# A hybrid decoder block on one core: every large SBUF tile moved to an address that is a multiple of 512 bytes

## The chip, the core and the metric

The kernel runs on 1 core of one Trainium2 chip (trn2). The metric is device microseconds of one execution. TensorE (PE) multiplies, VectorE (DVE) and ScalarE (ACT) prepare operands and empty PSUM, GpSimd (POOL) and SyncE (SP) mostly issue DMAs. SBUF has 128 partitions; a tile takes the same byte range in each of them, and "address" below is the byte offset in a partition.

## What is computed

The reference, cut to what matters (256 tokens, model width 4096):

```python
h = rmsnorm(x, norm_w)
proj = h @ w_in                                   # (256, 4096) x (4096, 20480)
u_p, z_p, u_c, b_c, c_c, z_c, g_logit = split(proj)
y_pool = causal_multiscale_pool(u_p, pool_w, pool_scale) * silu(z_p)
y_conv = b_c * conv3(c_c * u_c) * silu(z_c)
br = stack([y_pool, y_conv]) @ w_branch           # two products (256, 2048) x (2048, 4096)
merged = sum(sigmoid(g_logit + gate_b) * br)
out = rmsnorm(x + merged @ w_out, final_norm_w)
```

Everything is float32 in and out. The weights, 446 loads of 1 MB each, are read once.

## The kernel before, in words

**Precision.** Each operand is split in two float32r parts, a high part (the rounded value) and a low part (the rest). A product of two float32 matrices is three matmuls: high x high, high x low, low x high. Each matmul has a 128x128 float32r stationary operand (512 bytes per partition, loaded by its own weight-load instruction, PEld in the profile) and a 128x512 float32r moving operand (2,048 bytes per partition).

**Units and steps.** The work is a list of units of 1,024 output columns: 20 units over `w_in` (units `c..`, `p..`, `g..`), 8 over `w_branch` (`b..`), 4 over `w_out` (`o..`). A unit is a list of steps of 256 rows of contraction; each step loads one 1 MB weight block. A step is of kind P (plain: 8 products, 24 matmuls) or S (a Strassen-like scheme with 7 products, 21 matmuls, for which VectorE makes sums of weight quarters). A string such as `TEN` or `NINE` (lines 34 to 49) gives a unit's kinds in order. Two more kinds, B and M, serve the causal pooling.

**The tiles that matter here.**

- `raw` (line 100): three slots of 8 KB, the weight blocks as they come from HBM through SP's queue.
- `ring` (line 99): 15 cells of 4 KB, each a high and a low half of 2,048 bytes. ACT writes the high half (`highs`, line 223), DVE the low half (`lows`, line 227), from `raw` or from `parts`. Matmuls read `ring` as the moving operand.
- `parts` (line 1136): the sums of quarters of an S step, made by DVE.
- `arena` (line 98): the stationary operands, in entries of 512 bytes (`Operand`, line 167). What does not fit there lies in three other tiles: `last_pair` (the pair of rows that is `LAST`, line 144), `side` (the first four S entries of a pair that is held as a P operand but that some units use in an S step, line 193) and, in the first unit alone, `extra` (line 138).
- `E` and `Y` (lines 101, 102): results of a unit on their way through sums, gates and transposes; `sa` and `sb` scratch; `ident` the identity for transposes; `bands`, `edge` the moving operands of the pooling matmuls, with `cnt` and `ic` their counts; small tables `par`, `rin`, `rout`, `ssq`, `ossq`.

**Order.** All engines run in the order in which the program is written (`pin`, line 57). While the matmuls of step i are issued (`multiply`, line 1020), the preparations of up to four later steps are issued between them (`pump`, line 987), as far as `raw` slots and `ring` cells are free; results of the unit before come one piece at a time (`tick`, line 1013). A matmul waits for its ring cell and, for the first product into a PSUM bank, for the bank to have been emptied; ACT waits for a ring cell to be released by the matmuls that read it; DVE waits for ACT's high half.

**Placement.** SBUF pools are stacks from the two ends. Pool `const` (line 89) takes tiles from the left end, which begins at 16,512 behind a reserved stretch and four constants; pool `upper` (line 90) from the right end, which lies at 229,344. `opening`, `parts`, `side`, `bands`, `more` are opened behind `const` one after another, `last` (which holds `last_pair`) left of `upper`. Each tile is rounded up to 32 bytes. Nothing in the kernel states an address; they follow from the order in which tiles are made.

Of the kernel before, what the change touches and what calls it, by code (L numbers as in the profile page):

```python
# [9 lines left out]
F32 = mybir.dt.float32  # L10
F32R = mybir.dt.float32r
# [4 lines left out]
P = 128  # L16
T = 256
D = 4096
HALF = D // 2
NU = 1024  # L20
NH = 512
EPS = 1e-6
WINDOWS = (2, 4, 8, 16)
KB = 256

ND, NS, NB = 8, 6, 2
CELLS = 15
NRAW = 3
# [24 lines left out]
def hybrid_block(ctx: ExitStack, tc: tile.TileContext, x, xc, prm, rows_in, w_in, pool_w, w_branch, w_out, out):  # L53
# [5 lines left out]
    def act(dst, src, func=AF.Copy, **kw):  # L59
        return pin(nc.scalar.activation(dst, src, func, **kw))  # L60
# [4 lines left out]
    def mul(dst, a, b):  # L65
        return tt(dst, a, b, ALU.mult)
# [16 lines left out]
    def move(dst, src):  # L83
        return pin(nc.gpsimd.dma_start(dst, src))
# [5 lines left out]
    upper = ctx.enter_context(tc.tile_pool(name="upper", bufs=1, side="right"))  # L90
# [2 lines left out]
    dram = ctx.enter_context(tc.tile_pool(name="dram", bufs=1, space=bass.MemoryType.DRAM))  # L93

    def sb(name, shape, dt=F32):
        return const.tile(shape, dt, name=name)

    arena = sb("arena", [P, (4 * ND + 7 * NS + 8 * (NB - 1)) * KB], F32R)
    ring = sb("ring", [P, CELLS, 2, NH], F32R)
    raw = upper.tile([P, NRAW, 2 * NU], F32, name="raw")  # L100
    E = sb("E", [P, 2, NU])
    Y = upper.tile([P, 2, NU], F32, name="Y")
    sa = sb("sa", [P, 8, P])
    ident = sb("ident", [P, P])
    par = sb("par", [P, 112])
    rin = sb("rin", [P, 3])
    rout = sb("rout", [P, 2])
    ssq = sb("ssq", [P, 2, 4])
    ossq = sb("ossq", [P, 2, 5])

    PE_ = [[psum.tile([P, NH], F32, name=f"sums{t}{n}") for n in range(2)] for t in range(2)]
    PF = [psum.tile([P, NH], F32, name=f"shared{i}") for i in range(4)]
# [28 lines left out]
    band_pool = {}  # L141
# [81 lines left out]
    def highs(cells, src):  # L223
        for i, c in runs(cells):
            act(ring[:, c, 0], src[:, i])

    def lows(cells, src):
        for i, c in runs(cells):
            sub(ring[:, c, 1], src[:, i], ring[:, c, 0].bitcast(F32))

    def high(cell, a=0, b=NH):
        return ring[:, cell, 0, a:b]

    def low(cell, a=0, b=NH):
        return ring[:, cell, 1, a:b]

    def quarters(tile_):
        return tile_.rearrange("p a (b c) -> p (a b) c", c=NH)

    class Step:  # L240
# [28 lines left out]
        def rest(self):  # L269
# [32 lines left out]
            if self.kind == "B":  # L302
                def parts(cells):
                    self.cells = cells
                    highs(cells, quarters(E))
                    lows(cells, quarters(E))

                return [(4, lambda: self.unit.flags.get("base"), parts)]

            def pooled(cells):  # L310
                self.pool_cells = cells
                q = quarters(E)[:, 2 * self.g:2 * self.g + 2]
                highs(cells, q)
# [5 lines left out]
        def groups(self):  # L319
            gs = []  # L320
            if self is steps[0]:
                for k in (1, 0):
                    for n in (1, 0):
                        cell = self.cells[2 * (1 - k) + 1 - n]
                        h, l = high(cell), low(cell)
                        for i in range(3):
                            for t in range(2):
                                ah, al = self.op.standing(k, t)
                                gs.append([("E", t, n), [((ah, h), (al, h), (ah, l))[i]], ()])
                        gs[-1][2] = [cell]  # L330
            elif self.kind == "P":
                for k in (1, 0):
                    for n in reversed(self.halves):
                        cell = self.cells[2 * (1 - k) + 1 - n]
                        for t in self.toks:
                            ah, al = self.op.standing(k, t)
                            gs.append([("E", t, n), [(ah, high(cell)), (ah, low(cell)), (al, high(cell))], ()])
                        if self.final:
                            gs[-1][2] = [cell]
            else:  # L340
                d, w = self.cells, self.sum_cells
                prods = {"M1": (A11, d[2], ("F", 0, 0)),
                         "N3": (Q3, d[1], ("E", 0, 0)),
                         "M2": (A12, d[0], ("E", 0, 1)),
# [107 lines left out]
    def transposes(src, done):  # L452
        items = []
        for j in range(4):
            def f(j=j):
                for i in range(2):
                    for t in range(2):
                        c = (2 * j + i) * P
                        pin(nc.tensor.transpose(shared(j)[:, i * T + t * P:i * T + (t + 1) * P],  # L459
                                                src[:, t, c:c + P], ident))  # L460
                done(j)
            items.append(f)
        return items
# [4 lines left out]
    def put(dst, src):  # L468
        for k in range(2):
            move(dst[:, :, 1 - k], src.rearrange("p (q k) t -> p q k t", k=2)[:, :, k])  # L470

    def chan(tile_):
        return tile_.rearrange("p a n -> p (a n)").rearrange("p (b t) -> p b t", t=T)

    def bankview(j):
        return shared(j).rearrange("p (b t) -> p b t", t=T)

    def gap(n):
        return [None] * n
# [38 lines left out]
    def in_unit(name, col, epi, text, **kw):  # L518
        units.append(Unit(name, lambda i: w_in[col // NU, i], seq_x(text), x_ops, epi, scaled=True, **kw))
        units[-1].text = text  # L520
        return units[-1]
# [15 lines left out]
    def silu_y(late):  # L537
        def silu(t):
            act(Y[:, t], Y[:, t], AF.Silu, **(dict(scale=rin[:, t:t + 1]) if late else {}))
        return gap(18 if late else 3) + [lambda: silu(0), None, lambda: silu(1)]  # L540
# [5 lines left out]
    def conv_units(c, first):  # L546
        base = 2 * HALF + c * NU

        def b_epi(u):
            def copy(j):  # L550
                act(chan(Y)[:, 2 * j:2 * j + 2], bankview(j))
            return gap(6) + transposes(E, copy) + [lambda: move(g_d[c], Y)]

        def c_epi(u):
# [5 lines left out]
            def taps(j):  # L560
                v, y = chan(E)[:, 2 * j:2 * j + 2], chan(Y)
                for i in range(2):
                    b = 2 * j + i
                    kb = 8 * c + b
                    act(y[:, b], v[:, i], AF.Identity, scale=tap_col(2, kb), bias=bias_col(kb))
                for s in (1, 2):
                    for i in range(2):
                        b = 2 * j + i
                        kb = 8 * c + b
                        stt(y[:, b, s:], v[:, i, 0:T - s], tap_col(2 - s, kb), y[:, b, s:], ALU.mult, ALU.add)  # L570

            items = gap(6) + pairs(transposes(E, copy)) + gap(1)
            for j, n in enumerate((1, 7, 8, 8)):
                items += gap(n) + [lambda j=j: taps(j)]
            return items + [lambda: move(E, g_d[c])] + gap(6) + [lambda: mul(E, E, Y), lambda: put(y_d[1, c], chan(E))]

        u = in_unit(f"cz{c}", base + 3 * HALF, lambda u: silu_y(u.late) + (gap(4) + side_items(ND - 1) if first else []),
                    FIRST if first else SIX4, dst=Y)
        u.rotates, u.late = first, not first
# [10 lines left out]
    def band_items(c):  # L590
        if c == 0:
            side["stack"].close()
            pool = bands_open.enter_context(tc.tile_pool(name="bands", bufs=1))
            band_pool.update(cnt=pool.tile([P, 2], F32, name="cnt"),
                             bands=pool.tile([P, 2, T], F32R, name="bands"),
                             edge=pool.tile([P, 2, P], F32R, name="edge"),
                             ic=pool.tile([P, 16], F32, name="ic"))
            for t in range(16):
                pin(nc.gpsimd.memset(band_pool["ic"][:, t:t + 1], 1.0 / (t + 1)))
        cnt, bands, edge = (band_pool[k] for k in ("cnt", "bands", "edge"))  # L600

        def scratch(g):
            return sa[:, 4 + 2 * g:6 + 2 * g].rearrange("p o c -> p (o c)")

        def select(q, pattern, base, mult):
            pin(nc.gpsimd.affine_select(out=q, in_=q, pattern=pattern, base=base, channel_multiplier=mult,
                                        compare_op=ALU.is_ge, fill=0.0))

        def trailing():
            for g in range(2):  # L610
                w, q = WINDOWS[2 * c + g], scratch(g)[:, 0:P]
                pin(nc.gpsimd.memset(q, 1.0))
                select(q, [[-1, P]], 0, 1)
                select(q, [[1, P]], w - 1, -1)

        def counts():
            for g in range(2):
                pin(nc.vector.tensor_reduce(out=cnt[:, g:g + 1], in_=scratch(g)[:, 0:P], axis=mybir.AxisListType.X,
                                            op=ALU.add))
            pin(nc.vector.tensor_scalar(out=cnt, in0=cnt, scalar1=-1.0, scalar2=None, op0=ALU.mult))  # L620

        def leading():
            for g in range(2):
                w, q = WINDOWS[2 * c + g], scratch(g)
                pin(nc.gpsimd.memset(q, 1.0))
                select(q, [[1, T]], 0, -1)
                select(q, [[-1, T]], w - 1, 1)

        def finished():
            for g in range(2):  # L630
                w, q = WINDOWS[2 * c + g], scratch(g)
                stt(edge[:, g], ident, -float(w), q[:, 0:P], ALU.mult, ALU.add)
                stt(bands[:, g, 0:P], ident, cnt[:, g:g + 1], q[:, 0:P], ALU.mult, ALU.add)
                pin(nc.vector.tensor_copy(bands[:, g, P:T], q[:, P:T]))

        return [trailing] + gap(4) + [counts, leading] + gap(4) + [finished]
# [611 lines left out]
```

## Time and profile before

| | us |
|---|---|
| median of 3 runs | 2374.27 |
| lowest, highest run | 2373.22, 2375.88 |
| profiled execution, whole | 2374.06 |
| profiled execution, span of the program's instructions | 2372.2 |
| granted TensorE clock in that span | 0.998 |

The profile page gives busy time by engine, then the chain of work that ended last. The groups of instructions name the tiles that an instruction writes and reads (`sums<-ring,arena`: output in PSUM tile `sums`, moving operand from `ring`, stationary operand from `arena`). In a group's row the last two numbers before the second bar are the total busy time in us and the mean duration of one instruction in ns. Matmuls are pipelined, so the duration of one is not its cost: the cost is the distance from one start to the next, which is read from the timeline. A row of the timeline has the start of a run of like instructions, its length, engine, line, form, and xN instructions; start of the next row minus start of this row, divided by N, is the pitch.

### The profile page before, as it was taken

To read this page: it belongs to the slowest core of one execution; us is meant where nothing else is said; L and a number is where in the kernel's file an instruction comes from. 1 tells how busy PE (TensorE), PEld (TensorE's weight loads), DVE (VectorE), ACT (ScalarE), POOL (GpSimd) and SP (SyncE) were. 2 spreads that over 40 slices of the span, in tenths; PEclk is the share of its full clock that TensorE was granted. 3 is DMA by queue.
4 is the path that set the end of the run, shared out by engine and by line. 5 is a ranking of instruction groups with operands and counts; after the bars stand their busy time and mean duration, and the time that the engine had idled before them with its cause. 6 is when DMAs were issued, how large, how long until landed. Compare 5 with 4: busy or idle time off the path is not lost.

```text
span 2372.2 us, 28256 instructions
## 1 busy us (share of the span) xinstructions
PE 2355.7 (99%) x10457; PEld 1944.9 (82%) x10457; DVE 2185.2 (92%) x2389; ACT 1525.0 (64%) x1804; POOL 124.4 (5%) x188
## 2 busy tenths in 40 slices
PE   9999999999999999999999999999999999999997
PEld 7888888888888888888888888888888888888886
DVE  8889989989989969969999999998898799899998
ACT  6666656656656556657667767666665666566664
POOL 0000000000001000100100000001100000000000
PEclk9999999999999999999999999999999999999999
DMA  9656646756747646746877787778766766767876
GB/s 345 230 202 234 222 166 258 238 189 236 230 178 262 217 178 217 239 167 229 287 241 249 256 264 240 247 268 278 267 253 241 248 237 238 256 215 266 270 253 265
DMA packets 93098, 567.87 MB, mean 239 GB/s; under 512 B 10208, under 2 KB 10464, under 8 KB 32032
## 3 DMA queue, kind: packets, MB, share of 16 engines
q1 hardware_dynamic: 69824, 485.39, 56.4%
q0 software_dynamic: 22560, 79.44, 12.9%
q8 instruction: 82, 1.34, 0.2%
q10 hardware_dynamic: 576, 1.24, 0.1%
q14 instruction: 56, 0.46, 0.1%
HBM read 523.03 MB, written 27.26 MB: 232 GB/s over the span
## 4 chain that ended last, share of the span: by engine, by line
PE 95%; DVE 3%; ACT 1%; DMA 1%; issue 0%; SPq 0%; DVEq 0%; ACTq 0%
PE sums L1025 69%; PE shared L1025 23%; DVE ring L63 1%; PE shared L670 1%; PE shared L459 1%; DVE parts L63 1%; DVE E L63 1%; DMA raw<-in_w_in_dram 1%; ACT ring L60 0%; DVE raw L63 0%; DVE E L75 0%; DMA raw<-in_w_out_dram 0%; ACT E L60 0%; ACT raw L60 0%; PE shared L646 0%
## 5 line engine op out<-in xcount | busy, mean ns | idle before, releaser
L1025 PE MATMUL sums<-ring,arena 128*128 128x512 f32 x7179 | 1679.1, 390 | 3.0 <-ACT E L60 1.4
L1025 PEld LDWEIGHTS sums<-ring,arena 128*128 128x128 f32 x7179 | 1346.5, 188 | 284.9 <-ACT E L60 2.4
L63 DVE TENSOR_TENSOR ring<-raw,ring 128x1024 fp32r<-128x1024 f32 (+3 forms) x877 | 972.8, 1130 | 123.2 <-ACT ring L60 121.6
L60 ACT ACTIVATE ring<-raw 128x1024 fp32r<-128x1024 f32 (+3 forms) x678 | 794.6, 1206 | 255.4 <-PE sums L1025 97.4
L60 ACT ACTIVATE ring<-parts 128x512 fp32r<-128x512 f32 (+1 forms) x647 | 483.4, 761 | 471.6 <-DVE parts L63 410.4
L1025 PE MATMUL shared<-ring,arena 128*128 128x512 f32 x2175 | 524.6, 389 | 0.0
L63 DVE TENSOR_TENSOR ring<-parts,ring 128x1024 fp32r<-128x1024 f32 (+1 forms) x449 | 500.1, 1161 | 6.2 <-ACT ring L60 6.1
L1025 PEld LDWEIGHTS shared<-ring,arena 128*128 128x128 f32 x2175 | 408.3, 188 | 84.9
L63 DVE TENSOR_TENSOR parts<-parts,raw 128x512 f32<-128x512 f32 x422 | 292.6, 693 | 0.0
L63 DVE TENSOR_TENSOR parts<-raw 128x1024 f32<-128x1024 f32 x211 | 258.6, 1225 | 9.2 <-DMA raw<-in_w_in_dram 5.2
L1025 PE MATMUL sums<-ring,last_pair 128*128 128x512 f32 x321 | 81.0, 396 | 0.0
L1025 PEld LDWEIGHTS sums<-ring,last_pair 128*128 128x128 f32 x321 | 60.4, 188 | 14.5 <-DVE ring L63 0.2
L1025 PE MATMUL shared<-ring,last_pair 128*128 128x512 f32 x204 | 50.6, 397 | 0.0
L1025 PEld LDWEIGHTS shared<-ring,last_pair 128*128 128x128 f32 x204 | 38.4, 188 | 9.3
L60 ACT ACTIVATE E<-sums 128x512 f32<-128x512 f32 x72 | 40.8, 594 | 5.9 <-PE sums L1025 3.4
L87 POOL DMA_DIRECT2D E<-Y x20 | 24.3, 1454 | 366.5 <-DVE Y L63 322.6
L1025 PE MATMUL shared<-ring,side 128*128 128x512 f32 x153 | 38.5, 396 | 0.0
L60 ACT ACTIVATE E<-sums,rin 128x512 f32<-128x512 f32 x28 | 17.7, 688 | 29.3 <-PE sums L1025 29.3
L1025 PEld LDWEIGHTS shared<-ring,side 128*128 128x128 f32 x153 | 28.8, 188 | 6.8
L60 ACT ACTIVATE Y<-shared 128x512 f32<-128x512 f32 x56 | 30.4, 602 | 4.1 <-PE shared L459 3.4
L63 DVE TENSOR_TENSOR E<-E,Y 128x2048 f32<-128x2048 f32 x13 | 29.8, 2292 | 0.9 <-ACT Y L60 0.7
L63 DVE TENSOR_TENSOR Y<-Y 128x512 f32<-128x512 f32 (+1 forms) x33 | 28.7, 869 | 1.7 <-ACT Y L60 0.2
(133 smaller groups left out, 711.8 us busy)
## 6 DMA issues: line engine op xcount, KB each, us to landing
raw<-in_w_in_dram SPq DMA_DIRECT2D x318, 1024.0 KB, 4.9
raw<-in_w_branch_dram SPq DMA_DIRECT2D x64, 1024.0 KB, 4.9
raw<-in_w_out_dram SPq DMA_DIRECT2D x64, 1024.0 KB, 5.0
E<-Y POOLq DMA_DIRECT2D x20, 512.0 KB, 8.3
E<-in_rows_dram POOLq DMA_DIRECT2D x16, 512.0 KB, 8.5
gates_d<-E POOLq DMA_DIRECT2D x8, 1024.0 KB, 6.0
Y<-E POOLq DMA_DIRECT2D x10, 512.0 KB, 8.2
y_d<-E POOLq DMA_DIRECT2D x8, 512.0 KB, 6.5
```

Source lines behind the costliest of these rows:

```text
L60: return pin(nc.scalar.activation(dst, src, func, **kw))
L63: return pin(nc.vector.tensor_tensor(out=dst, in0=a, in1=b, op=op))
L87: return pin(nc.gpsimd.dma_start(dst, src, accum_op=ALU.add))
L459: pin(nc.tensor.transpose(shared(j)[:, i * T + t * P:i * T + (t + 1) * P], src[:, t, c:c + P], ident))
L670: pin(nc.tensor.matmul(o, a, b, start=(k, i) == (0, 0), stop=(k, i) == (3, 2)))
L1025: pin(nc.tensor.matmul(ps, lhs, rhs, start=n == 0, stop=n == u.total[b] - 1))
```

## The change

No instruction is added, removed or moved; sizes, engines, queues and waits are the same. Tiles are placed elsewhere.

```diff
     def sb(name, shape, dt=F32):
+        return upper.tile(shape, dt, name=name)
+
+    def blocks(name, shape, dt=F32):
         return const.tile(shape, dt, name=name)
-    arena = sb("arena", [P, (4 * ND + 7 * NS + 8 * (NB - 1)) * KB], F32R)
-    ring = sb("ring", [P, CELLS, 2, NH], F32R)
-    raw = upper.tile([P, NRAW, 2 * NU], F32, name="raw")
-    E = sb("E", [P, 2, NU])
-    Y = upper.tile([P, 2, NU], F32, name="Y")
-    sa = sb("sa", [P, 8, P])
-    ident = sb("ident", [P, P])
+    blocks("front", [P, 96])
+    arena = blocks("arena", [P, (4 * ND + 7 * NS + 8 * (NB - 1)) * KB], F32R)
+    ring = blocks("ring", [P, CELLS, 2, NH], F32R)
+    E = blocks("E", [P, 2, NU])
+    sa = blocks("sa", [P, 8, P])
+    ident = blocks("ident", [P, P])
+    raw = sb("raw", [P, NRAW, 2 * NU])
+    Y = sb("Y", [P, 2, NU])
     par = sb("par", [P, 112])
...
     ossq = sb("ossq", [P, 2, 5])
+    sb("back", [P, 40])
...
-            band_pool.update(cnt=pool.tile([P, 2], F32, name="cnt"),
-                             bands=pool.tile([P, 2, T], F32R, name="bands"),
+            band_pool.update(bands=pool.tile([P, 2, T], F32R, name="bands"),
                              edge=pool.tile([P, 2, P], F32R, name="edge"),
+                             cnt=pool.tile([P, 2], F32, name="cnt"),
                              ic=pool.tile([P, 16], F32, name="ic"))
```

`front` (384 bytes) moves everything behind it in `const` on by 384. The small tables leave `const`, and with the ones made later (`rin_m`, `root` and the like) go to `upper`; `back` (160 bytes) fills these up so that they and it take 992 bytes, as far as the right end of a multiple of 512. `cnt` moves behind `bands` and `edge`. The addresses, from the sizes:

| tile | address before | mod 512 | address after | mod 512 |
|---|---|---|---|---|
| arena | 16,512 | 128 | 16,896 | 0 |
| ring | 100,480 | 128 | 100,864 | 0 |
| E | 161,920 | 128 | 162,304 | 0 |
| sa | 170,112 | 128 | 170,496 | 0 |
| ident | 174,208 | 128 | 174,592 | 0 |
| extra, parts | 175,552 | 448 | 175,104 | 0 |
| side, sb | 183,744 | 448 | 183,296 | 0 |
| bands | 183,776 | 480 | 183,296 | 0 |
| edge | 185,824 | 480 | 185,344 | 0 |
| last_pair | 188,384 | 480 | 187,392 | 0 |
| raw | 196,576 | 480 | 195,584 | 0 |
| Y | 221,152 | 480 | 220,160 | 0 |

Distances among `arena`, `ring`, `E`, `sa` and `ident` are the same before and after. `side` ends at 187,392, where `last_pair` begins: nothing is left free there.

## The prediction

> **What bounds the kernel now.** First the page's busy times and the chain that ended last.
>
> ```profile
> PE 2355.7 (99%) x10457; PEld 1944.9 (82%) x10457; DVE 2185.2 (92%) x2389; ACT 1525.0 (64%) x1804; POOL 124.4 (5%) x188
> ...
> PE 95%; DVE 3%; ACT 1%; DMA 1%; issue 0%; SPq 0%; DVEq 0%; ACTq 0%
> ```
>
> The end is set by matmuls that follow one another without a gap, for 95% of the chain. So what counts is the number of matmuls and their pitch; VectorE at 92% stands close behind. Next the groups by form, for the stationary operand each kind reads:
>
> ```profile
> L1025 PE MATMUL sums<-ring,arena 128*128 128x512 f32 x7179 | 1679.1, 390 | 3.0 <-ACT E L60 1.4 <-DVE ring L764 1.0 <-DVE ring L63 0.6
> L1025 PE MATMUL shared<-ring,arena 128*128 128x512 f32 x2175 | 524.6, 389 | 0.0
> L1025 PE MATMUL sums<-ring,last_pair 128*128 128x512 f32 x321 | 81.0, 396 | 0.0
> L1025 PE MATMUL shared<-ring,last_pair 128*128 128x512 f32 x204 | 50.6, 397 | 0.0
> L1025 PE MATMUL shared<-ring,side 128*128 128x512 f32 x153 | 38.5, 396 | 0.0
> L1025 PE MATMUL sums<-ring,side 128*128 128x512 f32 x51 | 14.7, 396 | 0.0
> L1025 PE MATMUL sums<-ring,extra 128*128 128x512 f32 x36 | 10.4, 396 | 0.0
> ```
>
> The same matmul is shown 6 to 8 ns longer when its weights come from last_pair, side or extra: 321 + 204, 153 + 51 and 36, together 765, against 9,354 from arena. A duration is no pitch, so the timeline of TensorE, at one P step and at runs of one kind in S steps:
>
> ```profile
> 77.70 7.87 PE L1025 MATMUL sums<-ring,arena 128*128 128x512 f32 x34
> 85.41 5.78 PE L1025 MATMUL sums<-ring,last_pair 128*128 128x512 f32 x24
> 91.02 1.32 PE L1025 MATMUL sums<-ring,arena 128*128 128x512 f32 x5
> ```
>
> From arena (85.41 - 77.70) / 34 = 226.8 ns, from last_pair (91.02 - 85.41) / 24 = 233.8 ns.
>
> ```profile
> 1188.37 2.98 PE L1025 MATMUL shared<-ring,last_pair 128*128 128x512 f32 x12
> 1191.18 0.86 PE L1025 MATMUL sums<-ring,last_pair 128*128 128x512 f32 x3
> 1191.88 6.32 PE L1025 MATMUL sums<-ring,arena 128*128 128x512 f32 x27
> 1198.03 0.86 PE L1025 MATMUL sums<-ring,side 128*128 128x512 f32 x3
> ...
> 1361.40 2.26 PE L1025 MATMUL shared<-ring,side 128*128 128x512 f32 x9
> 1363.50 6.29 PE L1025 MATMUL sums<-ring,arena 128*128 128x512 f32 x27
> 1369.63 0.86 PE L1025 MATMUL sums<-ring,side 128*128 128x512 f32 x3
> ```
>
> From last_pair again (1191.18 - 1188.37) / 12 = 234.2, from side (1363.50 - 1361.40) / 9 = 233.3. The arena matmuls right behind a stretch from last_pair take (1198.03 - 1191.88) / 27 = 227.8, those behind side (1369.63 - 1363.50) / 27 = 227.0: the slow state outlasts its cause by a few matmuls.
>
> The trace shows no addresses; the table of tiles has them. Arena and ring stand at 128 past a multiple of 512, both. Extra and side stand at 448, last_pair at 480. So the matmul is fast where weights and moving operand have the same place in a 512-byte block, and 7 ns slower in each of the three tiles where they differ. What else the slow tiles have in common I can't find: they are read by the same instructions, in P and in S steps, into both kinds of bank, in early and late units. I take the place of the weights relative to the moving operand as the cause, or their place in a 128-byte block, which makes the same forecast: arena and ring are multiples of 128 now, the three others are not.
>
> **The change, part by part.**
>
> The 765 slow matmuls. All PE operands come to 0 of 512, so weights and ring agree as arena and ring do now, and the pitch should become arena's. Last_pair: 525 x (234.0 - 226.8) = 3.8 us. Side: 204 x (233.3 - 226.8) = 1.3. Extra, taken like last_pair by its equal 396 ns: 36 x 7 = 0.25. Sum 5.4 us.
>
> The after-effect. Some 525 / 22 = 24 stretches from last_pair, each followed by 27 x (227.8 - 226.8) = 0.03 us, and 17 steps with side (12 of their 21 matmuls), each with two returns of 27 x 0.2 = 0.005: 0.7 + 0.2 = 0.9 us. Together 6.3 us of matmul time.
>
> How much of it reaches the end. Where the slow matmuls lie, and how busy DVE is there:
>
> ```profile
> 1170.00:1730.00 560.00, 36.22 (x150) 28.24 (x150) 0.00 (x0) 2.13 (x4) 0.00 (x0) 1.00 0.79 261
> ...
> 1170.00:1730.00 560.00, 34.41 (x132) 24.84 (x132) 0.00 (x0) 0.00 (x0) 3.38 (x6) 1.00 0.79 261
> ...
> 1200.00:1600.00 400.00, 400.00 (x1758) 329.78 (x1757) 396.25 (x437) 279.94 (x331) 26.29 (x30) 1.00 0.78 254
> 1600.00:1730.00 130.00, 130.00 (x574) 107.33 (x572) 116.72 (x132) 88.65 (x103) 15.21 (x23) 1.00 0.83 279
> ```
>
> The first row counts last_pair's instructions, the second side's (first number PE), the others all: 150 + 132 = 282 of the 765 are in the gate units, some 2.3 us of the gain with its after-effect, and from 1200 to 1600 DVE has only 400 - 396.25 = 3.75 us free. DVE follows TensorE there (ring cells must be released first), and between 1600 and 1730 it has 13 us free, so it can move up; I take off 0.2 us. A last stretch from last_pair lies where the chain is on DVE:
>
> ```profile
> 2306.49 0.69 DVE ring L63
> ...
> 2339.54 4.71 DMA raw<-in_w_out_dram
> ...
> 2340.20 2.98 PE L1025 MATMUL shared<-ring,last_pair 128*128 128x512 f32 x12
> ```
>
> Its 21 matmuls (0.2 us) gain nothing. So 6.3 - 0.4 = 5.9 us reach the end.
>
> The 9,354 arena matmuls and 96 that read ring on both sides. Arena and ring move together by 384, so their relative place stays; the trace has no matmul whose operands stand at 0 of 512, so the cost of that is bounded by the nearest rows. Above: the pitch of the slow tiles, +7 ns, 9,354 x 7 = +65 us. Below: the opening matmuls show 2.04 us for 4 and 2.90 for 6 of the same form, 430 ns each; half of that, 215, is what a matmul would take at an exactly doubled rate, 11.7 ns under today's:
>
> ```profile
> 6.17 2.04 PE L1025 MATMUL sums<-ring,arena 128*128 128x512 f32 x4 [1.03 <-DVE ring L764]
> ...
> 6.17 2.90 PE L1025 MATMUL sums<-ring,arena 128*128 128x512 f32 x6 [1.03 <-DVE ring L764]
> ```
>
> I take nothing: the only pair of places that runs at 226.8 is an equal one, and it stays equal.
>
> VectorE and ScalarE. raw moves from 480 to 0, parts from 448 to 0, E from 128 to 0. Rows of one shape with sources at 480 and 128:
>
> ```profile
> L63 DVE TENSOR_TENSOR ring<-raw,ring 128x1024 fp32r<-128x1024 f32 x513 | 616.6, 1226 | 12.3 <-ACT ring L60 11.8
> L63 DVE TENSOR_TENSOR ring<-E,ring 128x1024 fp32r<-128x1024 f32 x4 | 4.8, 1220 | 0.0
> L60 ACT ACTIVATE ring<-raw 128x1024 fp32r<-128x1024 f32 x333 | 337.1, 1052 | 27.3 <-PE sums L1025 16.5 <-issue 4.2 <-PE shared L1025 3.4
> L60 ACT ACTIVATE ring<-E 128x1024 fp32r<-128x1024 f32 x4 | 4.2, 1059 | 3.3 <-DVE E L75 2.5 <-PE sums L1025 0.8
> ```
>
> 6 ns less and 7 ns more, from four cases each. Over about 900 such DVE operations that is 5 us either way, behind matmuls for all but the last 66 us, from 2306 on, where the chain is on DVE: 0.5% of that is 0.3 us either way. I take nothing.
>
> DMA. Loads into raw (480) land in
>
> ```profile
> raw<-in_w_in_dram SPq DMA_DIRECT2D x318, 1024.0 KB, 4.9
> ...
> E<-in_x_dram POOLq DMA_DIRECT2D x3, 1024.0 KB, 5.5
> ```
>
> 4.9 us against 5.5 into E (128), another queue. The chain gives DMA 1%, 24 us; that ratio, 12%, either way would be 3 us. I take nothing: the misplaced tile has the shorter row. `cnt` behind `bands` and the tables on the right change only addresses.
>
> The sum: 2374.06 - 5.9 = 2368.2 us. The profiled execution, 1.9 us over its span, lies 0.2 under the median of the runs.
>
> [...]
>
> **The rivals.**
>
> Nothing arrives, 2373. Either the three tiles are slow for another reason, or the gate units' gain is used up at the wait that ends them, where TensorE stands for 1.4 us until ACT empties a bank:
>
> ```profile
> 1726.69 3.56 PE L1025 MATMUL sums<-ring,arena 128*128 128x512 f32 x15
> 1731.67 0.51 PE L1025 MATMUL sums<-ring,arena 128*128 128x512 f32 x1 [1.41 <-ACT E L60]
> ```
>
> If DVE and ACT did not move up by 1730, all that was gained before would be waited there, and only the 87 + 24 slow matmuls behind 2100 would be left, of which 21 don't count: 90 x 7 = 0.6 us, hence 2373. Against it: DVE's 13 free us before 1730. The rows for these stretches, DVE alone in the first, last_pair and side in the others:
>
> ```profile
> 0.00:1070.00 1070.00, 955.33 (x1067) 1.00 0.63 223
> ...
> 2100.00:2372.20 272.20, 21.00 (x87) 16.31 (x87) 1.22 (x1) 0.00 (x0) 0.00 (x0) 0.99 0.76 256
> ...
> 2100.00:2372.20 272.20, 6.26 (x24) 4.51 (x24) 0.69 (x1) 0.62 (x1) 0.00 (x0) 0.99 0.76 256
> ```
>
> In the first 1,070 us DVE is free for 115, which leaves it room to follow.
>
> All matmuls become faster, 2275. If the place in the 512-byte block is what costs time, 128 is as wrong as 480, only less, and every pitch falls to 215: 10,119 x 11.7 = 118 us of matmuls. DVE would not allow it all: from 1200 to 1600 only 3.75 us are free, the rest, some 1,970 us, gains 5%, about 95 us: 2374 - 99 = 2275. For it: 215 would be a round half of the opening's 430. Against it: places 448 and 480, so different from 128, cost only 7 ns more.
>
> ```profile
> core 0: 2372.2 us, clock 0.998
> ```
>
> [...]
>
> Slower, 2439. If 0 is a bad place, all matmuls of arena and ring take the pitch of the slow tiles, from the first steady step at 20 us on: +65 us. For it: nothing at 0 was ever measured. Against it: no row with equal places is slow.
>
> **How the numbers follow.** Forecast 0.68, nothing arrives 0.16, all faster 0.07, slower 0.09. The forecast's own range is 2366 to 2371: 1.5 us of after-effect and absorption either way and 1 us from the spread of the runs. The range 2364 to 2375 takes in the nothing case with the runs' spread and leaves out the two large ones, 0.16. A difference under 0.2% (4.7 us, so down to 2369.5) can't be told from none; the forecast stands 1.3 us beyond, and I give it three in four to be seen. Faster 0.68 x 0.75 + 0.07 = 0.58, same 0.17 + 0.16 = 0.33, slower 0.09.
>
> **What would show it.** Right: matmuls from last_pair and side at 389 or 390 ns in the groups, 24 of them in 5.44 us between starts, 27 arena matmuls behind them in 6.12; arena unchanged at 226.8; DVE, ACT and landing times within 1%. A longer wait than 1.4 us at the first `w_branch` unit would show the gain used up. Wrong: any pitch of arena other than 226.8, or last_pair still at 234.

## The result and the profile after

| | us |
|---|---|
| before, median of 9 runs | 2373.88 (2373.22 to 2377.56) |
| after, median of 9 runs | 2368.05 (2367.41 to 2369.07) |
| ratio, 95% interval | 0.9973 (0.9963 to 0.9984) |
| profiled execution after: span, clock | 2365.7, 0.998 |

5.8 us faster, 0.25%. The page's busy times and chain, of the changed kernel:

```profile
PE 2348.7 (99%) x10457; PEld 1944.0 (82%) x10457; DVE 2183.7 (92%) x2389; ACT 1525.1 (64%) x1804; POOL 134.5 (6%) x188
...
PE 95%; DVE 3%; ACT 1%; issue 0%; DMA 0%; DVEq 0%; SPq 0%; ACTq 0%
```

The same work, the same chain; TensorE's busy time is 7.0 us shorter (2355.7 before), DVE's 1.5 us (2185.2), ACT's is the same to 0.1 us (1525.0). The groups by form (total us, mean ns before the second bar):

```profile
L1030 PE MATMUL sums<-ring,arena 128*128 128x512 f32 x7179 | 1677.3, 390 | 2.8 <-ACT E L60 1.4 <-DVE ring L769 1.3
...
L1030 PE MATMUL sums<-ring,last_pair 128*128 128x512 f32 x321 | 79.1, 389 | 0.4 <-DVE ring L63 0.4
L1030 PE MATMUL shared<-ring,last_pair 128*128 128x512 f32 x204 | 49.0, 389 | 0.0
L1030 PE MATMUL shared<-ring,side 128*128 128x512 f32 x153 | 37.4, 389 | 0.0
...
L1030 PE MATMUL sums<-ring,extra 128*128 128x512 f32 x36 | 10.1, 389 | 0.0
```

The three slow tiles' 396 and 397 ns have become 389; arena's stay at 390. The timeline of TensorE at the places shown of before:

```profile
84.20 5.60 PE L1030 MATMUL sums<-ring,last_pair 128*128 128x512 f32 x24
89.64 1.52 PE L1030 MATMUL sums<-ring,arena 128*128 128x512 f32 x6
...
1184.51 2.88 PE L1030 MATMUL shared<-ring,last_pair 128*128 128x512 f32 x12
1187.23 0.84 PE L1030 MATMUL sums<-ring,last_pair 128*128 128x512 f32 x3
1187.91 6.28 PE L1030 MATMUL sums<-ring,arena 128*128 128x512 f32 x27
1194.03 0.84 PE L1030 MATMUL sums<-ring,side 128*128 128x512 f32 x3
```

The pitches: last_pair (89.64 - 84.20) / 24 = 226.7 ns (233.8 before) and (1187.23 - 1184.51) / 12 = 226.7 (234.2); arena behind it (1194.03 - 1187.91) / 27 = 226.7 (227.8): the after-effect is gone with its cause.

How far the changed kernel is ahead near the end, read from the same rows in both. After:

```profile
2331.16 1.23 DVE L63 TENSOR_TENSOR ring<-raw,ring 128x1024 fp32r<-128x1024 f32 x1
...
2331.63 0.39 PE L1030 MATMUL sums<-ring,last_pair 128*128 128x512 f32 x1
...
2332.44 1.43 PE L1030 MATMUL sums<-ring,last_pair 128*128 128x512 f32 x5 [0.42 <-DVE ring L63]
...
2333.70 2.91 PE L1030 MATMUL shared<-ring,last_pair 128*128 128x512 f32 x12
```

Before:

```profile
2337.63 1.24 DVE L63 TENSOR_TENSOR ring<-raw,ring 128x1024 fp32r<-128x1024 f32 x1
...
2338.79 1.57 PE L1025 MATMUL sums<-ring,last_pair 128*128 128x512 f32 x6
2340.20 2.98 PE L1025 MATMUL shared<-ring,last_pair 128*128 128x512 f32 x12
```

The same matmul, the first of the last stretch from last_pair, starts 2338.79 - 2331.63 = 7.16 us earlier; six matmuls on, the lead is 2340.20 - 2333.70 = 6.50, and that is what the span shows (2372.2 - 2365.7). In between TensorE waits 0.42 us for a low half that DVE writes, and DVE's operation starts only 2337.63 - 2331.16 = 6.47 us earlier. Of the 7.16, 0.8 us is no part of the change: it is there at the first matmul whose weights have moved relative to ring. Before, and after it the changed kernel:

```profile
19.81 3.48 PE L1025 MATMUL sums<-ring,arena 128*128 128x512 f32 x14 [0.58 <-DVE ring L63]
...
23.13 0.86 PE L1025 MATMUL sums<-ring,extra 128*128 128x512 f32 x3
```

```profile
6.50 15.99 PE L1030 MATMUL sums<-ring,arena 128*128 128x512 f32 x63 [1.35 <-DVE ring L769]
22.32 0.84 PE L1030 MATMUL sums<-ring,extra 128*128 128x512 f32 x3
```

Up to there both run the same 63 matmuls from arena, in the same place relative to ring. In the execution of before TensorE waits once more among them, at 19.81, in that of after it doesn't, and the first matmul from extra starts 23.13 - 22.32 = 0.81 us earlier. That varies between executions, not with the addresses: in the twelve profiles of this study that matmul starts from 22.32 to 23.13, in the kernel with everything at 32 of 512 (below), which has no slow matmul either, at 22.98, and in the last kernel below, which has the addresses of the change, at 22.77. Without this the spans would be 6.5 - 0.8 = 5.7 us apart, as the medians are (5.83).

### The profile page after: what moved, and what is told of

Same layout as the page of the kernel before. It is cut to its first block, busy times and chain, and to the rows that moved or that the text cites. A ratio compares the mean times of both kernels' runs of the same rounds, so it can differ in the third digit from the quotient of the medians.

```text
span 2365.7 us, 28256 instructions
## 1 busy us (share of the span) xinstructions
PE 2348.7 (99%) x10457; PEld 1944.0 (82%) x10457; DVE 2183.7 (92%) x2389; ACT 1525.1 (64%) x1804; POOL 134.5 (6%) x188
## 4 chain that ended last, share of the span: by engine, by line
PE 95%; DVE 3%; ACT 1%; issue 0%; DMA 0%; DVEq 0%; SPq 0%; ACTq 0%
PE sums L1030 70%; PE shared L1030 23%; DVE ring L63 1%; PE shared L675 1%; PE shared L464 1%; DVE parts L63 1%; DVE E L63 1%; ACT ring L60 0%; DVE raw L63 0%; DVE E L75 0%; DMA raw<-in_w_out_dram 0%; DMA raw<-in_w_in_dram 0%; ACT E L60 0%; ACT raw L60 0%; PE shared L651 0%
```

## The experiments

The prediction left open what kind of place decides: relative or absolute, and in blocks of which size; whether the weights' tiles alone make the gain; and whether it could have been more. In all of these the program's instructions are those of the change; only addresses differ (but for the last one). "Distance" is the address of the weights minus that of the moving operand.

### The weights' tiles alone

Two pads added to the kernel before:

```diff
+    upper.tile([P, 88], F32, name="low")
     arena = sb("arena", ...)
...
     ossq = sb("ossq", [P, 2, 5])
+    sb("mid", [P, 48])
```

> The kernel before with last_pair, side and extra (and parts and bands with them) moved to 128 or 160 past a multiple of 512; arena, ring, E, sa at 128 and raw, Y at 480 stay. Theory A (the place of the weights relative to the moving operand in ring decides): matmuls from last_pair and side at 226.7 ns, 2368 us, the whole gain. Theory B (the gain came with raw, E and Y, through DVE, ACT or DMA): pitch of last_pair still 234, 2374 us.

Measured: 2367.74 us, ratio 0.9975 (0.9966 to 0.9985). Its timeline:

```profile
1184.39 2.88 PE L1027 MATMUL shared<-ring,last_pair 128*128 128x512 f32 x12
1187.11 0.84 PE L1027 MATMUL sums<-ring,last_pair 128*128 128x512 f32 x3
```

226.7 ns. The whole gain is there with raw, Y, E, arena and ring where they were: theory B falls (parts, which DVE writes, moves along here; in the kernel with last_pair alone, below, it doesn't). It is enough that the tiles which hold weights stand like ring; that this is 0 of 512 doesn't matter.

### Without the pad in front: last_pair 384 from ring

```diff
-    blocks("front", [P, 96])
```

> The changed kernel without the pad in front: arena, ring, E, sa, parts, extra and side at 128, last_pair, raw and Y at 0. If the places must agree modulo 512, last_pair (384 from ring) runs at 234 ns and the time is 2368 + 525 x 7.2 ns + 0.7 = 2372.5 us. If they must agree modulo 128 alone, all matmuls run at 226.7 and the time is 2368. A rule of absolute place (0 of 512 is best) would make arena slower than in the changed kernel; none is expected.

Measured: 2370.37 us, ratio 0.9987 (0.9978 to 0.9996).

```profile
1186.32 2.96 PE L1029 MATMUL shared<-ring,last_pair 128*128 128x512 f32 x12
1189.11 0.85 PE L1029 MATMUL sums<-ring,last_pair 128*128 128x512 f32 x3
...
L1029 PE MATMUL shared<-ring,side 128*128 128x512 f32 x153 | 37.4, 390 | 0.0
```

Last_pair runs at (1189.11 - 1186.32) / 12 = 232.5 ns; side in the same kernel, at distance 0, is shown with 390 ns in the groups (the last row), like arena. Agreement modulo 128 is not enough, although every tile is now a multiple of 128. The time is 2.3 us above that of the change, for 525 x 5.8 ns = 3.0 us of matmuls; the difference of 0.7 is within the spread of the runs.

### Everything at 32 of 512

```diff
-    blocks("front", [P, 96])
+    blocks("front", [P, 104])
...
-    sb("back", [P, 40])
+    sb("back", [P, 32])
```

> Every large tile at 32 past a multiple of 512, so that all weights agree with ring, and none is a multiple of 64. Relative place: all matmuls at 226.7 ns, 2368 us. Absolute place in a block of 64, 128 or 512 bytes: all 10,119 matmuls at 231 to 238 ns, 2368 + 71 = 2439 us.

Measured: 2369.48 us, ratio 0.9977 (0.9968 to 0.9987); ten runs, four of them from 2367.34 to 2368.14, six from 2369.30 to 2370.02. Its groups:

```profile
L1030 PE MATMUL shared<-ring,arena 128*128 128x512 f32 x2175 | 524.6, 390 | 0.0
L1030 PE MATMUL sums<-ring,last_pair 128*128 128x512 f32 x321 | 79.0, 390 | 0.0
```

No matmul is slow (390 or 391 ns in every group), with no tile at a multiple of 64: an absolute place does not decide, neither in blocks of 64 nor of 128 or 512. The profiled execution (2369.87 us) shows where the 2 us of its upper six runs may come from. A window of 3 us behind the wait that ends the gate units, here and in the changed kernel (columns: window, its length, busy us and count for PE, PEld, DVE, ACT, POOL, then granted clock, DMA share, GB/s):

```profile
1727.00:1730.00 3.00, 3.00 (x9) 2.32 (x8) 2.97 (x4) 2.75 (x4) 0.00 (x0) 0.50 0.91 380
```

```profile
1725.50:1728.50 3.00, 3.00 (x14) 2.42 (x15) 2.97 (x4) 3.00 (x5) 0.00 (x0) 1.00 0.89 369
```

9 matmuls instead of 14: behind that wait the granted clock was 0.50 over 3 us, against 1.00 in the changed kernel. The 30 matmuls that follow it take 8.68 us (row at the end), which at 226.7 ns each and 0.17 for the last one's tail would be 6.97: it costs 1.7 us. It is no effect of the pitch: in the groups no tile's matmuls are slow.

### 256 from ring

```diff
-    blocks("front", [P, 96])
...
     ident = blocks("ident", [P, P])
+    blocks("mid", [P, 64])
...
-    sb("back", [P, 40])
+    sb("back", [P, 72])
```

> Arena and ring at 128; side, extra, parts, last_pair, raw and Y at 384, 256 from ring. Agreement modulo 512 needed: 234 ns for the 765 matmuls, 2374 us. Modulo 256 or 128 enough: 226.7 ns and 2368 us. Below 226.7 would show that an equal place is not the best one.

Measured: 2369.49 us (one run, with a mean granted clock of 0.997 like the profile of the kernel at 32; its groups show the same wait with 1.9 us).

```profile
1185.07 2.88 PE L1030 MATMUL shared<-ring,last_pair 128*128 128x512 f32 x12
1187.79 0.84 PE L1030 MATMUL sums<-ring,last_pair 128*128 128x512 f32 x3
```

226.7 ns: a distance of 256 is as good as none. Agreement modulo 256 is enough here, 512 is not needed; modulo 128 was just seen to be too little (232.5 ns at 384).

### last_pair alone

One of those two pads, added to the kernel before:

```diff
+    upper.tile([P, 88], F32, name="low")
     arena = sb("arena", ...)
```

> The kernel before with last_pair alone moved, from 480 to 128, where arena and ring stand; side and extra stay at 448. If the tiles' costs add up, last_pair's matmuls go to 226.7 ns, side's and extra's stay at 233.8, and 3.8 us of the 5.9 come, with 0.7 of after-effect: 2369.4 us. If only all tiles together help, no gain: 2374.

Measured: 2369.94 us, ratio 0.9983 (0.9974 to 0.9992).

```profile
L1026 PE MATMUL shared<-ring,last_pair 128*128 128x512 f32 x204 | 49.0, 389 | 0.0
L1026 PE MATMUL shared<-ring,side 128*128 128x512 f32 x153 | 38.5, 396 | 0.0
```

With last_pair alone moved, its matmuls are fast and side's stay slow: each tile has its own cost. The medians give 3.8 us (2373.77 - 2369.94) for last_pair and 2.2 more with side and extra (2369.94 - 2367.74); the pitches give 525 x 7.3 = 3.8 us and 240 x 6.6 = 1.6, without the after-effect. The medians are too coarse for more: some runs of both kernels are longer at a mean granted clock of 0.997 (this kernel's profiled run, 2371.13 us, is one; its shorter runs show 0.998 or 0.999), and the lowest runs give 4.1 (2372.89 - 2368.77) and 1.7 (2368.77 - 2367.10).

### Three other distances

The changed kernel without the pad in front, with a pad of 16, 40 and 56 values in the middle and one of 0, 88 and 0 at the back; in the last one last_pair's view also starts 16 bytes into its tile. The first's edit:

```diff
-    blocks("front", [P, 96])
...
     ident = blocks("ident", [P, P])
+    blocks("mid", [P, 16])
...
-    sb("back", [P, 40])
```

> Arena and ring at 128; side and extra 64 from ring, last_pair 32. Agreement modulo 256: both slow, 230 to 240 ns, about 2374 us. If a difference that is a multiple of 64 (or of 32) were enough, side (or both) would run at 226.7.

> Side and extra 160 from ring, last_pair 192. Agreement modulo 256: both slow, 230 to 240 ns, about 2374 us. A pitch under 226.7 at any distance would point to a better place for arena itself.

> Side and extra 224 from ring, last_pair 16. Agreement modulo 256 to the byte: both slow, 230 to 240 ns. If a window of some tens of bytes around an equal place is enough, last_pair at 16 (and side at 224, 32 short of 256) runs at or near 226.7.

Measured, one run each: 2372.90, 2372.96 and 2370.97 us. The first of them, last_pair at 32, side at 64:

```profile
1187.18 2.96 PE L1029 MATMUL shared<-ring,last_pair 128*128 128x512 f32 x12
1189.98 0.86 PE L1029 MATMUL sums<-ring,last_pair 128*128 128x512 f32 x3
...
1360.14 2.26 PE L1029 MATMUL shared<-ring,side 128*128 128x512 f32 x9
1362.24 6.29 PE L1029 MATMUL sums<-ring,arena 128*128 128x512 f32 x27
```

The second, last_pair at 192, side at 160:

```profile
1186.67 2.91 PE L1030 MATMUL shared<-ring,last_pair 128*128 128x512 f32 x12
1189.42 0.85 PE L1030 MATMUL sums<-ring,last_pair 128*128 128x512 f32 x3
...
1359.53 2.27 PE L1030 MATMUL shared<-ring,side 128*128 128x512 f32 x9
1361.64 6.33 PE L1030 MATMUL sums<-ring,arena 128*128 128x512 f32 x27
```

The third, last_pair at 16, side at 224:

```profile
1185.21 2.88 PE L1029 MATMUL shared<-ring,last_pair 128*128 128x512 f32 x12
1187.93 0.84 PE L1029 MATMUL sums<-ring,last_pair 128*128 128x512 f32 x3
...
1357.65 2.26 PE L1029 MATMUL shared<-ring,side 128*128 128x512 f32 x9
1359.75 6.29 PE L1029 MATMUL sums<-ring,arena 128*128 128x512 f32 x27
```

Start to start, divided by 12 or 9, with the rows above and those of before (last_pair's 352 is 96 modulo 256; side's 320 is 64, and its 233.3 ns is what side has at a true 64):

| distance modulo 256 | 0 | 16 | 32 | 64 | 96 | 128 | 160 | 192 | 224 |
|---|---|---|---|---|---|---|---|---|---|
| pitch, ns | 226.7 | 226.7 | 233.3 | 233.3 | 234.2 | 232.5 | 234.4 | 229.2 | 233.3 |

None of these nine distances is better than 0, so none would be a better place for arena. 16 bytes on one side do no harm, 32 on either side do.

### arena itself 352 from ring

The suspected cost twelve times over.

```diff
-    blocks("front", [P, 96])
     arena = blocks("arena", ...)
+    blocks("gap", [P, 40])
     ring = blocks("ring", [P, CELLS, 2, NH], F32R)
...
-    sb("back", [P, 40])
+    sb("back", [P, 96])
```

> ring, side, extra, last_pair and all else at 288, arena alone at 128, 352 from ring, as far from it as last_pair was. The suspected cost, twelve times as often: if distance is the cause, the 9,354 matmuls from arena run at about 234 ns and the 765 others at 226.7, and the time is 2368 + 9,354 x 7.2 ns = 2435 us, less where VectorE already set the pace. If the place mattered only for these three tiles, 2368.

Measured: 2433.75 us, ratio 1.0252 (1.0238 to 1.0266). Groups and timeline:

```profile
L1030 PE MATMUL sums<-ring,arena 128*128 128x512 f32 x7179 | 1728.9, 397 | 2.7 <-DVE ring L63 1.6 <-DVE ring L769 0.9
L1030 PE MATMUL sums<-ring,last_pair 128*128 128x512 f32 x321 | 79.1, 390 | 0.0
```

```profile
1176.75 2.98 PE L1030 MATMUL shared<-ring,arena 128*128 128x512 f32 x12
1179.56 7.90 PE L1030 MATMUL sums<-ring,arena 128*128 128x512 f32 x33
```

The two tiles have changed roles: arena at 397 ns and a pitch of (1179.56 - 1176.75) / 12 = 234.2, last_pair at 390. 2433.75 - 2368.05 = 65.7 us for 9,354 matmuls are 7.0 ns each. That is the price seen on the three tiles' 765, over a twelvefold count. By the pitch it would be 234.2 - 226.7 = 7.5 ns; part of the missing 4.5 us is the wait of 1.41 us behind the gate units, which the slower TensorE no longer has, and where the rest goes was not followed. Arena stands here at 16,512, exactly where it stood in the kernel before, with a pitch of 226.8: it was ring that moved away by 160 bytes. The same weights at the same address are fast or slow by where the moving operand lies, which no rule of absolute place can give.

### The wait behind the gate units

The one stop of TensorE that the change left as it was; preparation is held back there.

```diff
-            after_group(u, g[0], st, st is u.steps[-1] and st.kind == "P" and 3 <= i < len(gs) - 1)
+            after_group(u, g[0], st, st is u.steps[-1] and (3 <= i < len(gs) - 1 if st.kind == "P" else u is last_x and i < 3))
```

> The changed kernel, with no preparation issued behind the first three products of the last step of the last gate unit, so that ACT empties the banks before it waits for sums of VectorE. If the queue order on ACT makes the wait of 1.8 us at the first w_branch unit, the wait shrinks to under 0.5 us and the time falls by 1 to 1.5 us, to 2366.8. If VectorE's lateness makes it, the wait turns up at a later matmul and the time stays at 2368.

Measured: 2368.34 us, ratio 0.9977 (0.9968 to 0.9986) to before, so no different from the change.

```profile
1725.63 1.66 PE L1030 MATMUL sums<-ring,arena 128*128 128x512 f32 x6 [1.44 <-ACT E L60]
```

The wait is still 1.44 us (1.41 without the edit, not the 1.8 of the expectation, which is that of the kernel at 32, 1.83). Holding back these three calls doesn't shorten it; that VectorE's lateness makes it is what is left of the two theories, but no run made VectorE earlier there.

## Why the prediction was right, point by point

- **The bound**: a chain of 95% matmuls, before and after. Right; wherever one of the three tiles' pitches changed, the time followed pitch times count to within about 1 us, once 1.7 us, what the clock of 0.50 cost the kernel at 32, are set aside where the mean granted clock was 0.997. With arena's pitch 65.7 us came of 9,354 x 7.5 ns = 70.
- **The 765 matmuls**, 5.4 us, and **the after-effect**, 0.9, together 6.3, of which 0.2 lie in the last 21 matmuls: 6.1 up to there. Measured: the lead of 7.16 us at 2331, less the 0.81 that the opening gave, is 6.35.
- **The cause.** "The place of the weights relative to the moving operand" held. Two details did not. The place counts modulo 256, not 512 (226.7 ns at 256 as at 0). And the alternative offered beside it as making the same forecast, a place in a 128-byte block, is wrong: at 32 of 512 nothing is slow (390 or 391 ns), and at 384 from ring, all multiples of 128, last_pair is (232.5 ns between starts).
- **What doesn't reach the end**, 0.4 us: measured 7.16 - 6.50 = 0.66. The place was named (the last stretch, where DVE sets the pace), but it was sized as the stretch's own 0.2 us; in fact it takes back part of what was gained before, since DVE is not earlier there by as much as TensorE. The gate units, where another 0.2 us was taken off, took nothing in this execution: the wait at their end is 1.41 us in both kernels. So up to the last stretch 6.35 us came where 5.9 were counted on, and there 0.66 went back where nothing was to. That the forecast of 5.9 lies within 0.1 of the 5.83 between the medians is in part luck: two errors of about half a microsecond cancel.

```profile
1725.32 0.98 PE L1030 MATMUL sums<-ring,arena 128*128 128x512 f32 x3 [1.41 <-ACT E L60]
```

- **The rival by which the gain is used up at that wait** did not come true in this execution. But the wait is not fixed: it is 1.4 us in the profiles of before (1.41), the change (1.41), the kernel without the pad in front (1.4) and the last one (1.44), and 1.8 to 2.0 in those of six others with the same instructions, among them one with the whole gain (the weights' tiles alone, 1.99) and one with about 1 us of it (distances 160 and 192, 1.82). So up to 0.6 us can go there; it doesn't follow the gain, and what decides it stays open.
- **arena's 9,354 matmuls unchanged**: right, 390 ns before and after; the rival that all become faster fell with it, and the table of distances shows no pitch under 226.7. Why the best pitch is 226.7 ns stays open; no address tried here changes it. The 215 ns of that rival, half of the opening's 430, was an estimate; no run shows it.
- **The slower rival**: its price was close (+65 us forecast for a bad place of arena, 65.7 measured when arena was put in one, at a somewhat higher pitch), its condition was not met: 0 is no bad place.
- **DVE, ACT, DMA at nothing**: right; the weights' tiles alone bring 2367.74 us. Loads into raw land in 4.8 us instead of 4.9, which is one step of the digit shown.

## What to carry to other kernels

Compare pitches by the tile that the weights come from, in a timeline, before looking for gaps: a tile that runs a few ns slower costs that on every matmul (233.8 against 226.8 ns from last_pair), and no wait shows it (0.0 us idle before last_pair's rows). Place weights and moving operand at the same address modulo 256 (float32r, 128x512: 226.7 ns at distances of 0, 16 and 256, 229.2 to 234.4 at the others tried); a common offset of 32 or 128 bytes did no harm here (390 or 391 ns, against 389 or 390 at 0). On this chain of matmuls the saving arrived whole (6.35 us), up to the first stage where another engine had no slack (0.66 went back).

## What was not expected

- The cost depends on the distance of two operands, alike at distances 256 bytes apart (226.7 ns at 0 and 256, 233.3 at 64 and 320), with no harm at 16 (226.7) and one milder place at 192 (229.2). Why the distance costs time, no run shows.
- In some profiles TensorE came back at about half its clock after the wait behind the gate units: in the kernel at 32, a wait of 1.83 us is followed by 3 us at a granted clock of 0.50 (window above), and 30 matmuls take 8.68 us; in that with the distances 160 and 192, a wait of 1.82 us by 3 us at 0.55. Over the whole span the profiles of these two and of three more (256 from ring, last_pair alone, 224 and 16), with waits of 1.8 or 1.9 us, show 0.997, the other seven 0.998 or 0.999.

```profile
1726.45 8.68 PE L1030 MATMUL sums<-ring,arena 128*128 128x512 f32 x30 [1.83 <-ACT E L60]
```

The kernel with the weights' tiles alone waited 1.99 us there, and the same 30 matmuls took 7.12 us, at a granted clock of 1.00 in the 3 us from 1726 on, so the length of the wait alone doesn't decide:

```profile
1725.78 7.12 PE L1027 MATMUL sums<-ring,arena 128*128 128x512 f32 x30 [1.99 <-ACT E L60]
```

What else decides, no run shows.
